# Gate stage of a decoder layer: the last chunk of each embedding product in column halves, a step's weights fetched a step sooner, another order in the last step

## The chip, the cores and the metric

The kernel runs on one core of one Trainium2 chip. The metric is the device time of one execution in microseconds (us); lower is better. TensorE (PE) multiplies matrices, VectorE (DVE) and ScalarE (ACT) do elementwise work, SyncE's queue (SP) issues the DMAs of the stage looked at here.

## The reference

One layer of a hybrid decoder, 512 tokens of width 1024, all in fp32. After a projection, an attention branch, a recurrence and their merge, the layer adds an output projection to the residual and then a gated embedding. The change touches only that last part:

```python
h = h + merged.astype(dt) @ w_out[i]
ple = (p[i] @ w_ple[i]).astype(f32) * jax.nn.sigmoid((h @ w_ple_gate[i]).astype(f32))
h = h + ple.astype(dt)
```

Here `p` is 512x256, `w_ple` 256x1024 and `w_ple_gate` 1024x1024.

## The kernel before, in words

Everything is kept transposed: 128 features on the partitions, 512 tokens along the free axis. An fp32 product is made of three passes in the faster float32r form: each operand is split into a high part (a rounded copy, made by ACT) and a low part (the rest, a subtraction on DVE), and TensorE sums high x high, high x low and low x high.

The **gate stage** is the loop at L1067. It takes the product of `h` with the gate weights by a 2x2 block scheme with seven block products in place of eight (Winograd's form of Strassen's). The two blocks of tokens are the column halves `left` and `right` of 256, the two blocks of the contraction are chunks 0 to 3 and 4 to 7, and each of the four steps `p` makes output chunks `p` and `p + 4`. In a step there are four PSUM banks `a`, `b`, `c`, `d` (tiles ga, gb, gc, gd in the trace) and seven calls of `product` (L1081), each with 12 matmuls over 256 columns: a, b, c, d, then the accumulating ones that I call a', c' and d' (the second into banks a, c and d). The sums of these blocks and the gates go through tiles `uv`, `sa` (output chunk p) and `sb` (output chunk p + 4) on DVE.

The **embedding product** of a step is `embed(0)` and `embed(1)` (L1077), one for each output chunk: two contraction chunks of 128, three passes each, so six matmuls over 512 columns into a bank `pe`. `gated` (L1093) multiplies the gate by `pe`, adds `hf` (the residual sum `h`), and issues the store of the output.

**Order.** TensorE's order is the program's. DVE, ACT and SP work of this stage passes through `arith`, `act` and `load`, and `pin` (L184) ties each such instruction behind the one before it on its engine: all three engines run in program order, and an instruction that waits holds up everything behind it on its engine. What is left over of a step (`rest`: the last gate of chunk p + 4 and both `gated`) is done in the next step. The last step (`last`, p = 3) has no next one: it makes the gates and stores half by half (L1151 to L1161).

**Weights.** `Quadrants(p)` holds a step's gate weights. Its method `first` loads 512 KB into a tile `gr` (L960), `second` loads two tiles of 256 KB, `gra` and `grb` (L965; for p = 0 one tile `gs` instead). `gr` has the tag `w` with two buffers: `gr` of step 2 takes the place of `gs`, and `gr` of step 3 the place of `gr` of step 1. `prepare` makes the block sums and the splits of the next step's weights (tiles `ws`, `gra`, `s1` to `s4`, `22`, `gwh`, `gwl` in the trace, an `h` or `l` behind the name for high and low) during the step before. `Embedding(p)` loads 256 KB of embedding weights into `pw` and splits them into `pwh` and `pwl`.

In step p the kernel before calls `Quadrants(p + 2).second()` and `Embedding(p + 2)` at the start (L1073, L1075), but `thirdW.first()` at the end (L1178), behind `rest[1]()` and `rest[2]()`, which issue the two stores of step p - 1.

Of the kernel before, what the change touches and what calls it, by code (L numbers as in the profile page):

```python
# [18 lines left out]
S = 512  # L19
# [41 lines left out]
def hybrid_layer_kernel(  # L61
# [16 lines left out]
    V, A, G, PE = nc.vector, nc.scalar, nc.gpsimd, nc.tensor  # L78
# [11 lines left out]
    def unit(tag, name, dt=F32, shape=(128, 512)):  # L90
        return sb.tile(list(shape), dt, tag=tag, bufs=BUFS[tag], name=name)

    def bank(tag, name):
        return psum.tile([128, 512], F32, tag=tag, bufs={"mm": 4, "g": 2, "a": 2}[tag], name=name)
# [12 lines left out]
    def run_due():  # L107
        again = True
        while again:
            again = False  # L110
            for s_ in list(sides):
                w = s_[0]
                if callable(w):
                    if not w():
                        continue
                elif w > now[0]:
                    continue
                again = True
                try:
                    y = next(s_[1])  # L120
                    s_[0] = y if callable(y) else now[0] + y
                except StopIteration:
                    sides.remove(s_)

    def tick(us):
        now[0] += us
        run_due()
# [121 lines left out]
    def mm3(ps, wh, wl, xh, xl, kn, us=0.227):  # L249
        n, tot = 0, 3 * kn  # L250
        for k in range(kn):
            for a, b in ((wh, xh), (wh, xl), (wl, xh)):
                PE.matmul(ps, a[:, k, :], b[k], start=(n == 0), stop=(n == tot - 1))  # L253
                n += 1
            tick(3 * us)
# [626 lines left out]
    for n in range(KD):  # L882
# [3 lines left out]
        h_ = unit("YB", f"mh{n}", R)  # L886
        l_ = unit("A", f"ml{n}", R)
# [6 lines left out]
    left, right, lo4, hi4 = slice(0, HALF), slice(HALF, S), slice(0, 4), slice(4, 8)  # L894

    def arith(dst, a, b, op):
        pin(V.tensor_tensor(dst, a, b, op=op))  # L897

    def add(dst, a, b):
        arith(dst, a, b, OP.add)  # L900

    def sub(dst, a, b):
        arith(dst, a, b, OP.subtract)

    def act(dst, src, f=AF.Copy, scale=1.0):
        pin(A.activation(dst, src, f, scale=scale), "A")
# [6 lines left out]
    def load(dst, src):  # L913
        pin(nc.sync.dma_start(dst, src), "S")
# [112 lines left out]
    ph, pl, pws = [], [], []  # L1027
    for at, n in enumerate(PAIRS):
# [24 lines left out]
        if at in (2, 3):  # L1053
            t = unit("A", f"pf{at}")
# [12 lines left out]
    for p in range(4):  # L1067
        pes = [bank("ag"[p % 2], f"pe{p}{i}") for i in range(2)]
        a, b, c, d = (bank("mm", f"g{i}{p}") for i in "abcd")
        uv, s0, s1 = (unit("YB", f"{i}{p}") for i in ("uv", "sa", "sb"))  # L1070
        u, v = uv[:, left], uv[:, right]
        last = p == 3
        thirdW = Quadrants(p + 2).second() if p < 2 else None  # L1073
        if p < 2:
            pws.append(Embedding(p + 2))  # L1075

        def embed(i, cols=slice(0, S)):  # L1077
            h_, l_ = pws[p].halves
            mm3(pes[i][:, cols], h_[:, i], l_[:, i], [t[:, cols] for t in ph], [t[:, cols] for t in pl], 2)

        def product(dst, i, j, begin=True):  # L1081
            n = 0
            for k in range(4):
                bh, bl = B[j][k]
                for wt, bt in ((W[i][0], bh), (W[i][0], bl), (W[i][1], bh)):
                    PE.matmul(dst[:, left], wt[:, k, :], bt, start=begin and n == 0, stop=n == 11, skip_group_check=not begin)
                    n += 1
            tick(1.36)

        def gate(s, sign, cols):  # L1090
            act(s[:, cols], s[:, cols], AF.Sigmoid, sign)

        def gated(s, i, cols=slice(0, S), p=p, pes=pes):  # L1093
            arith(s[:, cols], s[:, cols], pes[i][:, cols], OP.mult)
            add(s[:, cols], s[:, cols], hf[p + 4 * i][:, cols])
            load(out[p + 4 * i][:, cols], s[:, cols])

        def first_of_1(u=u, d=d, s1=s1):
            add(s1[:, left], u, d[:, left])
            gate(s1, -1.0, left)  # L1100

        def first_of_0():
            product(a, "12", "21", False)
            act(s0[:, left], a[:, left], AF.Sigmoid)

        def second_of_0():
            product(c, "s4", "22", False)
            add(s0[:, right], u, c[:, left])
            gate(s0, 1.0, right)

        def second_of_1():
            add(s1[:, right], v, d[:, left])
            gate(s1, -1.0, right)

        def prepare(what, *names):
            if not last:
                getattr(nextW, what)(*names)

        if p == 0:
            embed(0)  # L1120
            embed(1)
        else:
            rest[0]()
        product(a, "11", "11")
        act(u, a[:, left])
        prepare("highs", "22")
        prepare("sums", "s3", "s1")
        if p:
            prepare("sums", "s2")
        product(b, "s2", "t2")  # L1130
        sub(u, u, b[:, left])
        prepare("highs", "r0", "s1", "s3")
        if p:
            prepare("lows", "22")
            embed(1 if last else 0)
            if last:
                rest[1]()
        product(c, "s1", "t1")
        add(v, u, c[:, left])
        if last:  # L1140
            embed(0, right)
            rest[2]()
        elif p:
            embed(1)
        else:
            prepare("sums", "s2")
        prepare("highs", "s2")
        prepare("lows", "r0")
        product(d, "s3", "t3")
        second_of_1()  # L1150
        if last:  # L1151
            gated(s1, 1, right)
            second_of_0()
            gated(s0, 0, right)
            product(d, "22", "t4", False)
            first_of_1()
            gated(s1, 1, left)
            first_of_0()
            embed(0, left)
            gated(s0, 0, left)  # L1160
            break  # L1161
        prepare("lows", "s2", "s1")
        first_of_0()
        if p:
            rest[1]()
        second_of_0()
        prepare("sums", "s4")
        prepare("highs", "s4")
        prepare("lows", "s3")
        if p == 0:  # L1170
            prepare("lows", "22")
        prepare("lows", "s4")
        if p:
            rest[2]()
        if p < 2:
            pws[-1].high()
            pws[-1].low()
            thirdW.first()  # L1178
        product(d, "22", "t4", False)
        rest = (first_of_1, lambda s0=s0, gated=gated: gated(s0, 0), lambda s1=s1, gated=gated: gated(s1, 1))  # L1180
        W, nextW = nextW, thirdW
# [67 lines left out]
```

## Time and profile before

| | us |
|---|---|
| median of 3 runs (465.32 to 465.4) | 465.35 |
| the profiled execution's own time | 465.26 |
| its span, first to last instruction | 463.3 |
| start of the gate stage (first pe matmul) | 407.18 |
| start of the last step (its product a) | 445.63 |
| last matmul of the span starts | 458.55 |
| last DVE instruction starts | 460.24 |

Start times are counted from the start of the span. In a row of the timeline the columns are: start, duration, engine, line, operation, output<-inputs, shape, count; a bracket at the end gives the engine's idle time before the row and what ended it. The duration of a matmul is longer than its distance to the next one, because matmuls overlap: the pace is read from the starts. Nearly every DVE instruction of the stage has line L897 and every ACT instruction L906, the helpers, so tiles tell them apart, not lines.

### The profile page before, as it was taken

How to read it: one execution, taken by the hardware profiler on the slowest of the kernel's cores; microseconds unless marked ns; L12 is line 12 of the kernel's file. 1: busy time of each engine (PE TensorE's matmuls, PEld its weight loads, DVE VectorE, ACT ScalarE, POOL GpSimd, SP SyncE). 2: the span in 40 equal slices, each digit the busy share in tenths (PEclk: the TensorE clock that was granted, in tenths of full speed). 3: DMA queues.
4: the chain of work that ended last, by engine and by line, in shares of the span. 5: the costliest groups of instructions: out<-in, count | busy, mean ns of one | idle time of the engine just before them, and what ended most of it. 6: DMA issues, size and time to landing. Idle time of an engine off the chain costs nothing.

```text
span 463.3 us, 7630 instructions
## 1 busy us (share of the span) xinstructions
PE 456.1 (98%) x2882; PEld 385.1 (83%) x2882; DVE 352.4 (76%) x747; ACT 281.1 (61%) x506; POOL 13.2 (3%) x34
## 2 busy tenths in 40 slices
PE   8999999999999999999999999999999999999996
PEld 6888888888888888878887888888888888899995
DVE  4899568869979888987898575234559878898696
ACT  5856655667688876968686776465334444555331
POOL 1004000000000010000000000000000000000000
PEclk9999999999999999999999999999999999999999
DMA  7632223312433323131422333121324444380212
GB/s 242 224 137 90 93 94 104 118 49 97 153 92 127 125 58 121 73 115 48 115 91 92 115 91 115 46 69 47 113 76 142 169 129 157 123 273 3 91 42 95
DMA packets 19604, 50.43 MB, mean 109 GB/s; under 512 B 2416, under 2 KB 3312, under 8 KB 19568
## 3 DMA queue, kind: packets, MB, share of 16 engines
q1 hardware_dynamic: 19424, 49.95, 32.5%
q8 instruction: 22, 0.36, 0.3%
q14 instruction: 14, 0.11, 0.1%
q10 hardware_dynamic: 144, 0.01, 0.0%
HBM read 45.75 MB, written 2.10 MB: 103 GB/s over the span
## 4 chain that ended last, share of the span: by engine, by line
PE 88%; DVE 7%; DMA 2%; issue 1%; ACT 1%; SPq 0%; DVEq 0%; ACTq 0%
PE h L253 9%; PE gb L253 9%; PE ga L253 9%; PE ak L393 5%; PE ua L253 5%; PE bq L253 5%; PE ub L253 5%; PE bf L253 5%; PE aq L393 5%; PE ag L253 5%; PE bg L253 5%; PE av L393 5%; PE bi L393 4%; PE s L697 2%; PE pt L715 2%; DVE sa L897 1%
## 5 line engine op out<-in xcount | busy, mean ns | idle before, releaser
L236 ACT ACTIVATE wh<-wf 128x1024 fp32r<-128x1024 f32 (+1 forms) x70 | 67.3, 961 | 68.0 <-PE h L253 9.9
L237 DVE TENSOR_TENSOR wl<-wf,wh 128x1024 fp32r<-128x1024 f32 (+1 forms) x70 | 77.5, 1108 | 25.3 <-ACT wh L236 25.0
L253 PE MATMUL gb<-xh,wh 128*128 128x512 f32 x64 | 26.0, 407 | 0.0
L253 PE MATMUL ga<-xh,wh 128*128 128x512 f32 x64 | 25.7, 401 | 0.0
L253 PE MATMUL gb<-xh,wl 128*128 128x512 f32 x64 | 25.1, 393 | 0.0
L253 PE MATMUL gb<-xl,wh 128*128 128x512 f32 x64 | 25.0, 391 | 0.0
L253 PE MATMUL ga<-xh,wl 128*128 128x512 f32 x64 | 25.0, 391 | 0.0
L253 PE MATMUL ga<-xl,wh 128*128 128x512 f32 x64 | 25.0, 390 | 0.0
L253 PE MATMUL h<-mh,wh 128*128 128x512 f32 x64 | 24.9, 389 | 0.0
L253 PE MATMUL h<-mh,wl 128*128 128x512 f32 x64 | 24.9, 389 | 0.0
L253 PE MATMUL h<-ml,wh 128*128 128x512 f32 x64 | 24.9, 389 | 0.0
L704 DVE CUSTOM_DVE_ANT_0 p<-s,bias 128x128 f32<-128x128 f32 (+3 forms) x32 | 14.9, 485 | 12.9 <-PE s L697 12.9
L706 ACT ACTIVATE p<-p,ps 128x128 f32<-128x128 f32 (+3 forms) x32 | 17.7, 554 | 9.9 <-DVE ps L704 9.9
L719 ACT ACTIVATE ptS<-pt 128x384 f32<-128x384 f32 (+1 forms) x24 | 12.6, 523 | 11.8 <-PE pt L715 11.6
L253 PEld LDWEIGHTS gb<-xh,wl 128*128 128x128 f32 x64 | 12.0, 188 | 2.6
L253 PEld LDWEIGHTS ga<-xh,wl 128*128 128x128 f32 x64 | 12.0, 188 | 2.6
L253 PEld LDWEIGHTS h<-ml,wh 128*128 128x128 f32 x64 | 12.0, 188 | 2.6
L715 PE MATMUL pt<-ident,p 128*128 128x128 f32 x80 | 13.0, 276 | 1.1 <-DVE p L708 1.1
L253 PEld LDWEIGHTS h<-mh,wh 128*128 128x128 f32 x64 | 12.0, 188 | 2.5
L253 PEld LDWEIGHTS h<-mh,wl 128*128 128x128 f32 x64 | 12.0, 188 | 2.4
L253 PEld LDWEIGHTS ga<-xl,wh 128*128 128x128 f32 x64 | 12.1, 188 | 2.2
L253 PEld LDWEIGHTS ga<-xh,wh 128*128 128x128 f32 x64 | 12.0, 188 | 2.2
(411 smaller groups left out, 1403.4 us busy)
## 6 DMA issues: line engine op xcount, KB each, us to landing
wf<-in_w_tr_dram SPq DMA_DIRECT2D x32, 512.0 KB, 3.3
wf<-in_w_tok_dram SPq DMA_DIRECT2D x15, 512.0 KB, 3.3
wf<-in_w_up_dram SPq DMA_DIRECT2D x16, 256.0 KB, 2.5
wf<-in_w_o_dram SPq DMA_DIRECT2D x8, 512.0 KB, 3.3
bias<-in_brow_dram SPq DMA_DIRECT2D x8, 256.0 KB, 3.4
xres<-in_xT_dram SPq DMA_DIRECT2D x8, 256.0 KB, 3.0
gr<-in_w_g_dram SPq DMA_DIRECT2D x4, 512.0 KB, 4.7
xr<-in_xT_dram SPq DMA_DIRECT2D x7, 256.0 KB, 5.2
```

Source lines behind the costliest of these rows:

```text
L236: A.activation(hi, wraw[i], AF.Copy)
L237: pin(V.tensor_tensor(lo, wraw[i], hi.bitcast(F32), op=OP.subtract))
L253: PE.matmul(ps, a[:, k, :], b[k], start=(n == 0), stop=(n == tot - 1))
L393: PE.matmul(banks[t], a[:, s_], b[:, kk, :], start=(k == 0 and i == 0), stop=(k == KD - 1 and i == 2))
L697: PE.matmul(sp[:, o:o + nk], qn[h][:, qs], k_[:, :nk], start=(i == 0), stop=(i == 1))
L704: V.tensor_tensor_reduce(p_, sp[:, o:o + nk], T[:, nk - 1::-1], -1.0, 3e38, OP.add, OP.min, st[:, 0:1])
L706: A.activation(p_, p_, AF.Exp, bias=st[:, 0:1], scale=-1.0, accum_out=st[:, 1:2])
L715: PE.transpose(tp[:, kb * 128:kb * 128 + 128], pr[:, kb * 128:kb * 128 + 128], ident)
L719: A.activation(pt, tp[:, :n * 128], AF.Copy)
L897: pin(V.tensor_tensor(dst, a, b, op=op))
```

## The change: what it does

Three edits, all in the loop of the gate stage:

1. `embed` of a whole bank runs its first contraction chunk over 512 columns as before, and its second one over the left 256 columns (three passes) and then over the right 256 (three passes): nine matmuls in place of six. A call with one half given (`embed(0, right)`, `embed(0, left)`) does what it did.
2. `Quadrants(p + 2).first()` is called at the start of step p, ahead of `second()` and of `Embedding(p + 2)`, and no longer at its end.
3. In the last step TensorE's order a, b, E1, c, E0 right, d, c', d', a', E0 left becomes a, b, c, d, E1, c', d', E0 right, a', E0 left (E1 is `embed(1)`, E0 `embed(0)`). On DVE and SP `gated(s0, 0, right)` goes from before the last gate's sum (`first_of_1`) to behind it.

```diff
-        thirdW = Quadrants(p + 2).second() if p < 2 else None
+        thirdW = Quadrants(p + 2).first().second() if p < 2 else None
...
-        def embed(i, cols=slice(0, S)):
+        def embed(i, *parts):
+
             h_, l_ = pws[p].halves
-            mm3(pes[i][:, cols], h_[:, i], l_[:, i], [t[:, cols] for t in ph], [t[:, cols] for t in pl], 2)
+            for k in range(2):
+                for cols in parts or ((slice(0, S),), (left, right))[k]:
+                    for n, (wt, t) in enumerate(((h_, ph), (h_, pl), (l_, ph))):
+                        PE.matmul(pes[i][:, cols], wt[:, i, k, :], t[k][:, cols], start=k == n == 0,
+                                  stop=k == 1 and n == 2 and (bool(parts) or cols == right))
+            tick(1.36 if not parts else 0.68)
...
             prepare("lows", "22")
-            embed(1 if last else 0)
             if last:
                 rest[1]()
+            else:
+                embed(0)
         product(c, "s1", "t1")
         add(v, u, c[:, left])
         if last:
-            embed(0, right)
             rest[2]()
...
         second_of_1()
         if last:
+            embed(1)
             gated(s1, 1, right)
             second_of_0()
-            gated(s0, 0, right)
             product(d, "22", "t4", False)
             first_of_1()
+            embed(0, right)
+            gated(s0, 0, right)
             gated(s1, 1, left)
             first_of_0()
             embed(0, left)
...
             pws[-1].low()
-            thirdW.first()
         product(d, "22", "t4", False)
```

## Prediction

> **What bounds the kernel now.** I read the page first, then the chain that ended last from 400 us on, then the timelines of SP, PE and DVE through the gate stage. The page:
>
> ```profile
> span 463.3 us, 7630 instructions
> ...
> PE 456.1 (98%) x2882; PEld 385.1 (83%) x2882; DVE 352.4 (76%) x747; ACT 281.1 (61%) x506; POOL 13.2 (3%) x34
> ```
>
> TensorE is nearly always busy, with one weight load (PEld) for each matmul. So a change can save little more than PE's few gaps and what follows its last matmul. The chain gives PE's pace, and one stretch that isn't PE:
>
> ```profile
> 407.34 2.72 PE pe L253 x12
> ...
> 411.47 1.41 PE gb L1086 x12
> ...
> 435.03 0.34 SPq L914
> ...
> 435.43 3.66 DMA gr<-in_w_g_dram
> ...
> 439.18 0.70 DVE ws L897
> ```
>
> Pace: 2.72 / 12 = 0.227 us for a pass of 512 columns, 1.41 / 12 = 0.118 for one of 256; so a block product takes 1.41 and a whole embedding product 1.36. Further down, the end hangs on the load of step 3's `gr`: issued at 435.43 behind the store at 435.03, 3.66 us on the way, and DVE starts only then. DVE in order of time (the rows that I need):
>
> ```profile
> 428.37 0.42 DVE L897 TENSOR_TENSOR sb<-uv,gd 128x256 f32<-128x256 f32 x1 [1.22 <-PE gd L1086]
> ...
> 435.49 0.41 DVE L897 TENSOR_TENSOR sb<-uv,gd 128x256 f32<-128x256 f32 x1
> 439.18 0.69 DVE L897 TENSOR_TENSOR ws<-gr,gra 128x512 f32<-128x512 f32 x1 [3.28 <-DMA gr<-in_w_g_dram]
> ...
> 443.64 0.41 DVE L897 TENSOR_TENSOR sb<-uv,gd 128x256 f32<-128x256 f32 x1
> ...
> 446.51 0.41 DVE L897 TENSOR_TENSOR sa<-uv,gc 128x256 f32<-128x256 f32 x1
> ...
> 450.15 0.41 DVE L897 TENSOR_TENSOR sb<-uv,gd 128x256 f32<-128x256 f32 x1
> 451.33 0.42 DVE L897 TENSOR_TENSOR uv<-uv,gb 128x256 f32<-128x256 f32 x1 [0.76 <-ACT uv L906]
> ...
> 452.99 0.41 DVE L897 TENSOR_TENSOR uv<-uv,gc 128x256 f32<-128x256 f32 x1
> ...
> 454.64 0.41 DVE L897 TENSOR_TENSOR sb<-uv,gd 128x256 f32<-128x256 f32 x1
> 455.54 0.42 DVE L897 TENSOR_TENSOR sb<-sb,pe 128x256 f32<-128x256 f32 x1 [0.48 <-ACT sb L906]
> ...
> 456.34 0.41 DVE L897 TENSOR_TENSOR sa<-uv,gc 128x256 f32<-128x256 f32 x1
> 457.29 0.42 DVE L897 TENSOR_TENSOR sa<-sa,pe 128x256 f32<-128x256 f32 x1 [0.54 <-ACT sa L906]
> ...
> 458.09 0.41 DVE L897 TENSOR_TENSOR sb<-uv,gd 128x256 f32<-128x256 f32 x1
> 458.99 0.42 DVE L897 TENSOR_TENSOR sb<-sb,pe 128x256 f32<-128x256 f32 x1 [0.48 <-ACT sb L906]
> 459.44 0.43 DVE L897 TENSOR_TENSOR sb<-sb,hf 128x256 f32<-128x256 f32 x1
> 459.79 0.41 DVE L897 TENSOR_TENSOR sa<-sa,pe 128x256 f32<-128x256 f32 x1
> 460.24 0.42 DVE L897 TENSOR_TENSOR sa<-sa,hf 128x256 f32<-128x256 f32 x1
> ```
>
> DVE stands still for 3.28 us at 439.18 and is behind from there to the end. In step 1 it had waited 1.22 us for product d (428.37), so it was ahead of PE; in the last step it waits only for ACT's answers to its own sums (0.76, 0.48, 0.54, 0.48). PE beside it:
>
> ```profile
> 428.05 0.28 PE L1086 MATMUL gd<-tbh,s3l 128*128 128x256 f32 x1
> ...
> 440.66 0.28 PE L1086 MATMUL gd<-tbh,s3l 128*128 128x256 f32 x1
> ...
> 442.65 0.39 PE L1086 MATMUL gc<-hhh,s4h 128*128 128x256 f32 x1 [0.29 <-DVE uv L897]
> ...
> 445.63 0.28 PE L1086 MATMUL ga<-b11h,gwh 128*128 128x256 f32 x1
> ...
> 458.55 0.28 PE L253 MATMUL pe<-ph,pwl 128*128 128x256 f32 x1
> ```
>
> The last matmul of d starts at 428.05 and DVE reads d 0.32 later: I use 0.32 from the start of a bank's last matmul to its reader. In step 2 the reader comes at 443.64, 2.98 after 440.66. PE waits for DVE at 442.65, and after the last matmul (458.55) DVE still has 1.69 us to go until 460.24. So the last 25 us are bounded by DVE, late because of one load. The end follows the last DVE row by 463.3 - 460.24 = 3.06 us (store and close), which I keep.
>
> **The load of `gr` (edit 2).** What hinders an early load is its buffer, and what an early load may hinder stands behind it on SP:
>
> ```profile
> 409.53 0.37 SPq L914 DMA_DIRECT2D gr<-in_w_g_dram  x1
> 410.00 0.38 SPq L914 DMA_DIRECT2D gra<-in_w_g_dram  x1
> ...
> 411.38 0.33 SPq L914 DMA_DIRECT2D pw<-in_w_p_dram  x1
> ```
>
> ```profile
> 408.67 0.68 DVE L897 TENSOR_TENSOR 22l<-gs,22h 128x512 fp32r<-128x512 f32 x1
> ...
> 418.92 0.69 DVE L897 TENSOR_TENSOR ws<-ws,gr 128x512 f32<-128x512 f32 x1
> ...
> 422.26 0.69 DVE L897 TENSOR_TENSOR ws<-gr,gra 128x512 f32<-128x512 f32 x1
> ```
>
> ```profile
> 420.24 0.62 ACT L906 ACTIVATE pwh<-pw 128x512 fp32r<-128x512 f32 x1
> ...
> 432.82 0.61 ACT L906 ACTIVATE pwh<-pw 128x512 fp32r<-128x512 f32 x1
> ```
>
> ```profile
> DMA to landing us min/median/max: 5.7/6.3/6.5
> ```
>
> (The last line is that of the `grb` loads, the slowest of the stage.) `gr` of step 2 takes the buffer of `gs`, whose last reader ends at 408.67 + 0.68 = 409.35; it was issued at 409.53 already, and stays there. Now it goes first, and SP waits on it with `gra`, `grb` and `pw` of step 2 behind: the last goes out near 409.5 + 3 x 0.45 = 410.9 and is in by 417.4 even at 6.5 us. The first users are ACT at 420.24 (`pw`) and DVE at 422.26 (`gr`, `gra`): cover 2.8 and 4.9 us, so this costs nothing. `gr` of step 3 takes the buffer of step 1's, whose last reader ends at 418.92 + 0.69 = 419.61: issued near 419.7 in place of 435.43, with step 3's `gra`, `grb` and `pw` behind it until 421.1, all in by 427.6. ACT wants `pw` at 432.82, DVE wants `gr` at 435.83: covers of 5 and 8 us. Both stores of that step (the second at 435.03) now come behind these loads, which wait for nothing by then. So the 3.28 us stall goes.
>
> **What is late next, step 2.** Without the stall DVE goes on at 435.83 (435.49 plus the 0.34 that a short row takes when the next doesn't wait). From the stall's end to the sum from d it took 443.64 - 439.18 = 4.46, so it gets there by 440.3; what its rows there read from PE (b, c) and ACT is done before they come. Now d is late: PE's last matmul of d starts at 440.66 plus the price of edit 1. DVE reads d at 441.14 in place of 443.64: 2.50 earned, the rest of the 3.28 lost to waiting for PE.
>
> **Halves (edit 1).** A whole embedding product becomes 3 x 0.227 + 6 x 0.118 = 1.386 in place of 1.36: 0.026, and six of them (steps 0 to 2) before the last step make 0.16. No reader of `pe` comes so soon that a half done earlier helps it: the first one comes a step later, save in the last step. As bounds: nothing, if two halves run at 2 x 0.1135, and 3 x 0.188 us per product if the added weight loads lay open (a rival). I take 0.026, since each block product has 12 weight loads and 12 passes at the same 0.118.
>
> The Trainium skill (TensorE: Matmul & The Clock Gate, Back-to-back issue gap) gives N / 2.4 + 2.5 ns for a pass. By that a split adds 3 x 2.5 ns, 0.05 us over seven products and not 0.18, and the sum would come to 463.5; the trace's 227 and 118 ns are above its 216 and 109, and I go by the trace.
>
> **The last step.** PE without the wait at 442.65: a of step 3 starts at 440.82 + 0.118 + 3 x 1.413 = 445.18 (before 445.63, later by 0.61 of waiting). From there, by the new order: a, b, c, d end at 5.65, E1 at 7.04, c' at 8.45, d' at 9.87, E0 right at 10.57, a' at 11.99, E0 left at 12.69. The last matmul of each starts 0.12 before: d' 454.93, E0 right 455.63, a' 457.05, E0 left 457.75.
>
> DVE from 441.14, by the distances of the rows before (same instructions in the same order): the sum `sa` from c' of step 2 at +2.87, 444.01 (c' is readable at 440.82 + 24 x 0.118 + 0.32 = 443.97, so this just fits); `sb` at +6.51, 447.65; then from 450.15 as zero: `uv` from b +1.18, from c +2.84, `sb` from d +4.49 = 452.14, times `pe` +5.39 = 453.04 (E1 is done at 452.2), `sa` from c' +6.19 = 453.84 (c' readable at 453.83). All of it is ahead of d'. Now PE leads: `sb` from d' at 454.93 + 0.32 = 455.25 (DVE free since 454.2), `sa` times `pe` at 455.95, plus `hf` 456.41, `sb` times `pe` 456.75 (ACT's gate was ready at 455.25 + 0.90), plus `hf` 457.20, `sa` times `pe` at 457.75 + 0.32 = 458.07, plus `hf` at **458.52**. Before: 460.24. So edit 3 puts a DVE pair into ACT's pause after d', and DVE is free 0.5 us before the last multiplication: the end is PE-bound.
>
> **Sum.** 458.52 + 3.06 = 461.58 of span, 1.72 less; the execution 465.26 - 1.72 = 463.54, and against the median, 0.09 above that execution, **463.6**. In terms: 0.61 of PE's waits in step 2 gone, 0.16 of halves paid, the other 1.27 from the last step, where PE no longer waits and DVE no longer trails.
>
> **Rivals.**
>
> A: the load doesn't come sooner (its buffer or SP holds it to the old time) or another wait takes its place, and DVE reaches 450.15 as before. Then edit 3 alone acts: `uv` from c at 452.99 and `sb` from d at 454.64 hold c' and d' back as now, d' is read at about 456.8, `sa` times `pe` right at 457.4, E0 left starts its last matmul at 459.2, and the last row comes at 460.0: 465.1, no change. For it: DVE must still do as much. Against it: the buffer's reader ends at 419.61, 16 us before the old issue.
>
> B: the added weight loads lie open. One takes 188 ns:
>
> ```profile
> L253 PEld LDWEIGHTS pe<-ph,pwh x18: 187/188/192, 407.0 to 458.2; 128*128 128x128 f32 x18
> ```
>
> 21 of them (three in each of seven products) would cost 3.9 us on PE, and 463.6 - 0.2 + 3.9 = 467.3 comes out. It decides from 0.09 us per load on (1.9 / 21). Against it: block products with a 188 ns load for each pass go at 118 ns. The Trainium skill (TensorE: Matmul & The Clock Gate, The mechanism) says that weight loads overlap matmuls in flight only where their row groups differ, which would make this so; the trace doesn't bear it out for full 128 rows.
>
> C, slower too: SP waits for the buffer of `gs` with `pw` of step 2 behind it, and `pw` lands late. ACT then stands at 420.24, and behind it in order every gate and split of step 1. DVE makes up 1.22 (428.37) and the 3.28 of the stall that is gone; so the end is later only for a landing past about 425.2, 14 us after the issue. At 427 it would be 1.8 later less edit 3's 0.24, 466.9. Against it: 6.5 us is the longest landing.
>
> **How the numbers follow.** Forecast 0.84, A 0.10, B 0.03, C 0.03. The prediction is 463.6. Low end 463.2: the last step's 96 passes at half of 0.227 save 0.4. High end 464.6: a point between forecast and A, where some of DVE's 2.50 is lost to a wait that I don't see. A change under 0.2% (0.93 us) can't be told from none here: faster 0.84, same 0.10, slower 0.06.
>
> **What would show it.** In the changed profile: `gr` of step 3 issued near 419.7; DVE's wait before `ws` gone and one for PE before the sum from d at about 441.1; no wait of c' in step 2; a of the last step near 445.2; the last DVE row 0.77 after the last matmul's start, not 1.69; nine `pe` matmuls in about 1.39. Wrong if DVE waits for a DMA anywhere in the stage, if DVE is behind PE at d' of the last step, or if pe passes of 256 columns come slower than 0.118.

## The result, and the profile after

The changed kernel takes 462.29 us (median of 6 runs, 461.83 to 462.54) against 465.40 of the kernel before on the same chip: ratio 0.9932, 95% interval 0.992 to 0.9944. It is faster, as forecast, but by 3.1 us and not by 1.8: the time lies below the range on record.

The page of the changed kernel:

```profile
span 460.4 us, 7677 instructions
...
PE 454.5 (99%) x2903; PEld 384.7 (84%) x2903; DVE 352.2 (76%) x747; ACT 280.9 (61%) x506; POOL 13.1 (3%) x34
```

There are 21 matmuls more, three in each of seven embedding products, and yet PE's busy time is 1.6 us less. The SP queue's timeline:

```profile
409.39 0.33 SPq L914 DMA_DIRECT2D gr<-in_w_g_dram  x1
...
410.71 0.43 SPq L914 DMA_DIRECT2D pw<-in_w_p_dram  x1
...
419.50 0.33 SPq L914 DMA_DIRECT2D gr<-in_w_g_dram  x1
...
420.83 0.43 SPq L914 DMA_DIRECT2D pw<-in_w_p_dram  x1
```

These are the loads where the prediction put them (409.5, 410.9, 419.7 and 421.1), each within 0.3 us. DVE's timeline, the rows that answer to those of before:

```profile
435.10 0.41 DVE L897 TENSOR_TENSOR sb<-uv,gd 128x256 f32<-128x256 f32 x1
435.43 0.69 DVE L897 TENSOR_TENSOR ws<-gr,gra 128x512 f32<-128x512 f32 x1
...
440.36 0.42 DVE L897 TENSOR_TENSOR sb<-uv,gd 128x256 f32<-128x256 f32 x1 [0.39 <-PE gd L1092]
...
454.02 0.42 DVE L897 TENSOR_TENSOR sb<-uv,gd 128x256 f32<-128x256 f32 x1 [0.56 <-PE gd L1092]
454.80 0.42 DVE L897 TENSOR_TENSOR sa<-sa,pe 128x256 f32<-128x256 f32 x1 [0.35 <-PE pe L1083]
...
456.88 0.42 DVE L897 TENSOR_TENSOR sa<-sa,pe 128x256 f32<-128x256 f32 x1 [0.41 <-PE pe L1083]
457.33 0.42 DVE L897 TENSOR_TENSOR sa<-sa,hf 128x256 f32<-128x256 f32 x1
```

The 3.28 us stall before `ws` is gone, DVE waits for product d of step 2 instead, and in the last step for PE three times (d', E0 right, E0 left). The end is PE-bound: the last DVE row comes 0.84 us after the start of the last matmul (0.77 was forecast):

```profile
456.49 0.28 PE L1083 MATMUL pe<-ph,pwl 128*128 128x256 f32 x1
```

All of this is the walk on record, only earlier. How much earlier shows in the chain that ended last (start, us, what):

```profile
422.37 1.41 PE pe L1083 x9
423.78 1.38 PE gc L1092 x12
425.16 1.41 PE pe L1083 x9
426.57 1.38 PE gd L1092 x12
427.95 1.36 PE ga L1092 x12
```

A halved embedding product takes 1.41 us, about what was forecast (1.39). But a block product takes 1.36 to 1.38, where it took 1.41 before: 12 passes at 113 to 115 ns on average in place of 118. Nothing in the block products was edited.

To compare single profiles without the drift of the start, I use below the **stage length**: from the start of the first `pe` matmul to the start of the last DVE row. Before: 460.24 - 407.18 = 53.06. Forecast: 458.52 - 407.18 = 51.34. Changed: 457.33 - 407.15 = 50.18.

### The profile page after: what moved, and what is told of

Read it like the earlier page. It is cut to its first block, busy times and chain, and to the rows that moved or that the text cites. A ratio compares the mean times of both kernels' runs of the same rounds, so it can differ in the third digit from the quotient of the medians.

```text
span 460.4 us, 7677 instructions
## 1 busy us (share of the span) xinstructions
PE 454.5 (99%) x2903; PEld 384.7 (84%) x2903; DVE 352.2 (76%) x747; ACT 280.9 (61%) x506; POOL 13.1 (3%) x34
## 4 chain that ended last, share of the span: by engine, by line
PE 95%; DVE 2%; DMA 1%; SPq 0%; issue 0%; ACT 0%; DVEq 0%
PE h L253 9%; PE gb L253 9%; PE ga L253 9%; PE ak L393 5%; PE ua L253 5%; PE bq L253 5%; PE ub L253 5%; PE bf L253 5%; PE aq L393 5%; PE ag L253 5%; PE bg L253 5%; PE av L393 5%; PE bi L393 4%; PE pe L1083 2%; PE gc L1092 2%; PE gd L1092 2%
## 5 line engine op out<-in xcount | busy, mean ns | idle before, releaser
L253 PEld LDWEIGHTS gb<-xl,wh 128*128 128x128 f32 x64 | 12.1, 188 | 2.1
```

## The experiments

Each ran beside the kernel before on the same chip. That kernel's median differs a little from one group of runs to another (465.04 to 465.43), so each row has its own.

| run | us | before | ratio, 95% interval | stage length | block products (most) |
|---|---|---|---|---|---|
| changed kernel | 462.29 | 465.40 | 0.9932 (0.992 to 0.9944) | 50.18 | 113 |
| e1_no_halves | 463.05 | 465.04 | 0.9955 (0.9942 to 0.9967) | 51.20 | 118 |
| e2_halves_alone | 464.90 | 465.04 | 0.9999 (0.999 to 1.0008) | 52.74 | 113 |
| e3_load_alone | 463.23 | 465.04 | 0.9958 (0.9945 to 0.9972) | 51.33 | 118, from d of the last step on 113 |
| e4_order_alone | 465.05 | 465.04 | 0.9997 (0.9988 to 1.0005) | 53.02 | 118 |
| e5_first_chunk | 463.54 | 465.43 | 0.996 (0.9948 to 0.9973) | 51.52 | 118 |
| e6_last_pass | 462.25 | 465.43 | 0.9932 (0.992 to 0.9945) | 50.01 | 113 |
| e7_right_left | 462.12 | 465.43 | 0.993 (0.9918 to 0.9943) | 50.18 | 113 |
| e8_step0_only | 463.05 | 465.43 | 0.9957 (0.9943 to 0.997) | 50.83 | 113, then 118 |
| e9_load_halves | 462.48 | 465.12 | 0.9945 (0.9933 to 0.9958) | 50.46 | 113 |
| e10_last_384 | 462.38 | 465.12 | 0.9945 (0.9932 to 0.9957) | 50.37 | 113 |
| e11_other_passes | 463.26 | 465.12 | 0.9962 (0.9948 to 0.9975) | 51.20 | 118 |
| e12_first_twice | 463.88 | 465.12 | 0.9972 (0.9961 to 0.9982) | 51.90 | 118 |
| e13_all_halves | 462.28 | 465.17 | 0.9939 (0.9925 to 0.9952) | 50.32 | 113 |
| e14_first_cut | 462.43 | 465.17 | 0.9948 (0.9936 to 0.9961) | 50.53 | 113, c' and d' of the last step 118 |

The last column is the pace in ns per pass of the block products, from the starts in PE's timeline, once a run of passes has settled. In every run a' of the last step goes at 113; in the new order it stands directly behind E0 right, an embedding product in half columns.

### One edit taken away, one edit alone

**e1_no_halves**: edits 2 and 3 only.

```diff
-            for k in range(2):
-                for cols in parts or ((slice(0, S),), (left, right))[k]:
+            for cols in parts or (slice(0, S),):
+                for k in range(2):
```

> The changed kernel with edit 1 undone: each embedding product again six passes of 512 columns (load sooner and new order kept). Theory P (the halves change the pace: behind a product that ends in passes of 256 columns the block products go at 113 ns a pass, behind one that ends in passes of 512 at 118): block products back at 0.118, 28 x 12 x 0.0044 = 1.5 us more on PE less 0.2 for the halves: 463.4 to 463.6 us, the forecast's walk without its halves. Rival Q (the pace comes from the load or the order, or by chance from the layout of the code): pace stays 0.113, about 462.2 us. Rival R (halves only cost, 0.026 each, and PE's gain came from elsewhere): 462.1 us.

**e2_halves_alone**: the kernel before with the new `embed` and nothing else.

> The kernel before with edit 1 alone. Theory P: block products at 0.113 in all of the stage, but DVE still stands for the late load of gr, which hangs on the stores of step 1, and these come 0.4 us sooner as PE does: about 465.0 us (464.7 to 465.2), PE waiting for DVE in steps 2 and 3. Rival Q: pace 0.118, 465.5 us. Rival R: 465.4 to 465.6 us.

**e3_load_alone**: the kernel before with one call moved.

```diff
-        thirdW = Quadrants(p + 2).second() if p < 2 else None
+        thirdW = Quadrants(p + 2).first().second() if p < 2 else None
...
-            thirdW.first()
```

> The kernel before with edit 2 alone. All theories but Q: DVE's 3.28 us stall gone, pace 0.118, about 463.4 to 463.6 us by the same walk as the forecast's with the old order of the last step. Rival Q, if the load sets the pace: 462.2 us.

**e4_order_alone**: the kernel before with the last step's new order and products of whole passes.

> The kernel before with edit 3 alone (embedding products in passes of 512). The forecast's case A: DVE is as late as before, 0.24 us off the tail, 465.1 us, pace 0.118. Rival Q, if the order sets the pace: products of the last step at 0.113, but DVE-bound, 465.0 us.

**e9_load_halves**: edits 1 and 2 with the old order.

> Edits 1 and 2 with the old order of the last step. If the load and the halves are all that counts: as the changed kernel, within 0.2 us (3.1 under before). If the new order is needed once PE is quicker (the forecast's walk of the tail: DVE then has ACT's pause after d' to itself again): 0.2 to 0.5 us slower than the changed kernel.

Measured: without the halves 1.99 us under before, and the block products are back at 1.41, as the chain of e1_no_halves shows:

```profile
406.91 2.72 PE pe L1083 x12
409.63 1.41 PE ga L1091 x12
411.05 1.41 PE gb L1091 x12
```

Its stage length is 51.20; the walk on record without its halves gives 51.34 - 0.18 = 51.16. So the load and the order did what was forecast, and the whole miss is edit 1: 50.18 - 51.20 = -1.02 where +0.18 was forecast. Q and R fall.

The load alone gives 1.81 of these 1.99 us; the new order alone nothing that can be told from none, as case A had it (0.24 forecast). With the load, the new order takes another 0.13 off the stage without halves (51.33 to 51.20) and 0.28 with them (50.46 to 50.18, within the 0.2 to 0.5 expected of e9_load_halves). The DVE rows of the old order show why it gains less from a quicker PE; the first read of d in the last step and the last row, in e3_load_alone and then in e9_load_halves:

```profile
452.52 0.42 DVE L897 TENSOR_TENSOR sb<-uv,gd 128x256 f32<-128x256 f32 x1 [0.35 <-PE gd L1086]
...
458.12 0.42 DVE L897 TENSOR_TENSOR sa<-sa,hf 128x256 f32<-128x256 f32 x1
```

```profile
451.85 0.42 DVE L897 TENSOR_TENSOR sb<-uv,gd 128x256 f32<-128x256 f32 x1 [0.33 <-PE gd L1092]
...
457.44 0.42 DVE L897 TENSOR_TENSOR sa<-sa,hf 128x256 f32<-128x256 f32 x1
```

From d on the old order needs 5.60 and 5.59 us: DVE and ACT set the end, and the pace of c', d' and a' doesn't count. In the new order PE sets it. The differences of 0.13 and 0.28 are read in single profiles and are below what the medians can tell.

The halves alone are worth nothing, though the block products go at 113 there too: DVE's row in e2_halves_alone says why.

```profile
439.04 0.69 DVE L897 TENSOR_TENSOR ws<-gr,gra 128x512 f32<-128x512 f32 x1 [3.34 <-DMA gr<-in_w_g_dram]
```

With the load as late as before, the stage is DVE-bound from there on, and what PE gains it spends waiting for DVE. So the edits are not additive: 0 alone, 1.0 behind the load.

### What of the halves sets the pace

**e5_first_chunk**, **e6_last_pass** and **e7_right_left** change which passes of an embedding product are cut (k is the chunk, n the pass within it):

```diff
# e5_first_chunk
+ todo = [(0, n, c) for c in (left, right) for n in range(3)] + [(1, n, whole) for n in range(3)]
# e6_last_pass
+ todo = [(k, n, whole) for k in range(2) for n in range(3)][:5] + [(1, 2, left), (1, 2, right)]
# e7_right_left
+ todo = [(0, n, whole) for n in range(3)] + [(1, n, c) for c in (right, left) for n in range(3)]
```

> The changed kernel with the first chunk of each embedding product in halves and the second one whole: as many passes, but the last three before the block products are of 512 columns. Theory P1 (what stands last before the block products sets their pace): they go at 0.118, E0 right of the last step alone makes a' fast; about 463.2 us, 0.2 above e1_no_halves. Rival P2 (any passes of 256 columns in the embedding product do it, or a longer code): 0.113, 462.3 us. Rival L (layout of the code, the number of instructions): as P2, since it has the same number.

> The changed kernel with only the last of an embedding product's six passes in halves (seven matmuls in place of nine). P1: block products at 0.113, and 7 x 2 x 0.01 = 0.15 us less for halves: 462.1 us. If two passes of 256 columns are too few to set the pace (theory P3: some eight or nine are needed, since the first fast pass in the changed kernel is the tenth): 0.118 and 463.0 us. Rival L: pace could be either, since the number of instructions differs.

> The changed kernel with the halves in the other order, right before left. P1 and P2: no change, 462.3 us. Rival H (the pace comes from the half of the bank that was written last: right half, then the block product in the left half): pace 0.118, 463.2 us.

The chain of e5_first_chunk, and then that of e6_last_pass:

```profile
406.85 2.81 PE pe L1087 x18
409.66 1.42 PE ga L1096 x12
411.08 1.41 PE gb L1096 x12
```

```profile
407.18 2.76 PE pe L1087 x14
409.94 1.38 PE ga L1096 x12
411.32 1.36 PE gb L1096 x12
```

As many passes as in the changed kernel, but with the long ones last, leave the block products slow (P2 and L fall); one pass cut in two, if it is the last, makes them fast (P3 falls); the half that is written last doesn't matter (H falls). P1 stands as far as these three runs go: what counts is what stands just before the block products. e6_last_pass has the shortest stage, 0.17 less than the changed kernel, about the 0.15 that its 14 fewer matmuls were expected to save; by the medians the two can't be told apart.

**e8_step0_only** keeps the halves in step 0 and whole passes from step 1 on.

> The changed kernel with halves in step 0 alone, whole products of six passes of 512 columns from step 1 on. P1: the block products of step 0 and a, b of step 1 at 0.113, all from c of step 1 on at 0.118 again until E0 right of the last step: 9 x 12 x 0.0044 = 0.5 us better than e1_no_halves less 0.05 for halves, about 462.6 us. If the state once set is kept (theory P4): 0.113 to the end, 462.2 us.

```profile
420.69 1.36 PE gb L1096 x12
422.05 1.38 PE pe L1087 x6
423.43 1.41 PE gc L1096 x12
```

The rows are b of step 1, E0 with whole passes, and c: fast until the first pass of 512 columns, slow behind it. A fast state isn't kept (P4 falls); the stage is 0.37 shorter than that of e1_no_halves, where 0.45 was expected.

**e10_last_384** (the last pass as 384 and 128 columns), **e11_other_passes** and **e12_first_twice** (both from e1_no_halves):

```diff
# e10_last_384
+ todo = [...][:5] + [(1, 2, slice(0, 384)), (1, 2, slice(384, S))]
# e11_other_passes
-                for wt, bt in ((W[i][0], bh), (W[i][0], bl), (W[i][1], bh)):
+                for wt, bt in ((W[i][0], bh), (W[i][1], bh), (W[i][0], bl)):
# e12_first_twice, for the products behind an embedding product
+            if twice:
+                PE.matmul(dst[:, left], W[i][0][:, 0, :], B[j][0][0], start=True, stop=True)
```

> The changed kernel with an embedding product's last pass cut into 384 and 128 columns (as e6_last_pass with other widths). Theory W1 (any cut between the last pass of 512 columns and the block products breaks the slow pace): 113 ns, the same as e6_last_pass. Theory W2 (the pass before a block product must have its width, 256): 118 ns, 463.2 against 465.3 before.

> e1_no_halves with the three passes of a block product in another order (high x high, low x high, high x low), so that no weight is loaded twice running inside a chunk. If the slow pace comes from loading the same weight twice running: 113 ns in all block products and about 462.0 us. Else 118 ns and 463.1, as e1_no_halves (2.0 under before).

> e1_no_halves with the first pass of each block product that stands directly behind an embedding product given twice (five extra passes; the second one starts the sum anew, so the result is the same). Theory W1: an extra pass with the same weights between 512 columns and the rest breaks the slow pace: 113 ns in steps 0 to 2 and about 462.2 against 465.3 before. Theory W3 (only passes into the embedding's own bank do it): 118 ns, 463.1 plus 5 x 0.118 = 463.7.

The widths needn't match (W2 falls): 384 and 128 do it too, with a rougher first product (1.43). The order of the weights has no part in it. An extra pass of 256 columns behind the boundary changes nothing; the chain of e12_first_twice:

```profile
409.81 0.12 PE ga L1089
409.93 1.41 PE ga L1093 x12
411.34 1.41 PE gb L1093 x12
```

So W1 falls as it was put, and two readings were left: the short pass must be the embedding's (W3), or it must differ from the run of 256 columns that follows.

**e13_all_halves** (no pass of 512 columns in the stage) and **e14_first_cut** (whole embedding products, and the first pass of the block product behind each cut into 128 and 128 columns):

```diff
# e13_all_halves
+ todo = [(k, n, c) for k in range(2) for c in (left, right) for n in range(3)]
# e14_first_cut
+                    for q in (slice(0, 128), slice(128, HALF)) if cut and n == 0 else (left,):
```

> The changed kernel with both chunks of an embedding product in halves, twelve passes of 256 columns and no pass of 512 in the stage. Theory S (the slow pace is a state that the passes of 512 columns leave behind, and some nine short passes after a change of bank end it): block products at 113; the embedding's own passes begin at 118 and end at 113, 1.38 to 1.42 per product, about 462.3 (3.1 under before). Theory T (passes into the embedding's bank go at 118 whatever stands before): 12 x 0.118 = 1.42 per product, block products at 113, 462.4. If block products go at 118 again, three passes of 512 columns are needed ahead of the halves: 463.4.

> e1_no_halves with the first pass of each block product directly behind an embedding product cut into 128 and 128 columns. Theory W4 (any change of width to less than 256 columns between the 512 and the run of 256 ends the slow pace, whichever bank it writes): 113 in steps 0 to 2, about 462.2 (2.9 under before). Theory W3 (the short passes must stand ahead of the block product, as the last of the embedding's): 118, 463.1 to 463.3 (2.0 under before).

The chain of e13_all_halves and that of e14_first_cut:

```profile
407.18 2.87 PE pe L1087 x24
410.05 1.38 PE ga L1096 x12
411.43 1.36 PE gb L1096 x12
```

```profile
407.35 2.72 PE pe L1083 x12
410.07 1.48 PE ga L1092 x13
411.55 1.36 PE gb L1092 x12
```

In e13_all_halves the 24 short passes into `pe` go at 120 ns on average (2.87 / 24) and don't settle at 113: for them theory T holds, not S. The block products behind them are fast. In e14_first_cut the cut lies behind the boundary, in the block product's own bank, and the run behind it is fast (W4; W3 falls); c' of the last step, which was not cut, stays at 118. So neither the bank nor the place ahead of the boundary is needed. One rival is not separated: in every cut that worked, a short pass wrote columns that don't start at its bank's first one (the right half, the last 128 of 512, the second 128 of 256), while the extra pass of e12_first_twice wrote the same columns as the run behind it.

A cut isn't the only thing that changes the pace: a wait of PE can do it too. In e4_order_alone all embedding products of steps 0 to 2 are whole, and c' of step 2 comes after a wait for DVE (PE's timeline):

```profile
440.20 0.28 PE L1091 MATMUL ga<-hhh,gwh 128*128 128x256 f32 x1
...
441.50 0.28 PE L1091 MATMUL ga<-hhh,gwl 128*128 128x256 f32 x1
442.13 0.39 PE L1091 MATMUL gc<-hhh,s4h 128*128 128x256 f32 x1 [0.35 <-DVE uv L897]
...
442.70 0.28 PE L1091 MATMUL gc<-hhl,s4h 128*128 128x256 f32 x1
...
443.49 0.28 PE L1091 MATMUL gc<-hhh,s4l 128*128 128x256 f32 x1
443.61 0.37 PE L1091 MATMUL gd<-tbh,22h 128*128 128x256 f32 x1
443.81 0.28 PE L1091 MATMUL gd<-tbl,22h 128*128 128x256 f32 x1
...
444.99 0.28 PE L1091 MATMUL gd<-tbh,22l 128*128 128x256 f32 x1
```

a' goes at 118 ns (eleven distances in 1.30 us), c' settles at 113 (seven in 0.79), and d', whose second pass comes 0.20 us behind its first, is back at 118 (ten in 1.18, from 443.81 on). In the kernel before, the wait at 442.65 leaves the pace at 118. So a wait can end the slow pace, bring it back, or leave it; which of them isn't explained here. Where PE doesn't wait, all 16 traces keep to one rule: directly behind a pass of 512 columns the block products go at 118, behind a cut pass or an embedding product in half columns they settle at 113, and they stay there until the next embedding product.

## Why the prediction was wrong

**Right, with sizes.** The load: its queue slot, its buffer and its covers came within 0.3 us of the forecast, nothing behind it on SP came late (rival C didn't occur), and the load did not stay (rival A). The new bound: DVE waits for d in step 2, c' no longer waits, and the tail is PE-bound. Load and order together: 51.16 forecast, 51.20 measured in e1_no_halves. The added weight loads stay hidden: nine passes in 1.41 and not in 1.36 + 3 x 0.19 (rival B didn't occur). The Trainium skill (TensorE: Matmul & The Clock Gate, The mechanism) says that weight loads overlap matmuls in flight only where their row groups differ, and names beside it a background weight buffer that lets a load go ahead. No run here bears out the first as a limit: passes follow each other at 113 ns with a 188 ns load for each.

**Wrong: the step "Halves (edit 1)".** It gave the edit a price of 0.026 us per embedding product and no gain, "since each block product has 12 weight loads and 12 passes at the same 0.118", and took 0.118 as the block products' pace for the whole walk. The price held roughly: 1.386 forecast, 1.41 measured. The pace did not: the edit itself changes it. 28 block products at 1.36 (seven of them, each behind an embedding product, at 1.37 to 1.38) and not at 1.413 are 39.56 - (21 x 1.36 + 7 x 1.38) = 1.34 us less; seven embedding products cost 7 x 0.02 = 0.14 more than forecast; together 1.2, and the stage came out 51.34 - 50.18 = 1.16 shorter than forecast. The low end of the range allowed for passes at "half of 0.227" in the last step alone (96 passes, 0.4 us), so it ended at 463.2.

The trace before held the sign. In its last step, d and a' went at the fast pace (PE's timeline of the kernel before):

```profile
452.44 0.28 PE L1086 MATMUL gd<-tbl,s3h 128*128 128x256 f32 x1
...
453.23 0.28 PE L1086 MATMUL gd<-tbh,s3l 128*128 128x256 f32 x1
...
453.74 0.28 PE L1086 MATMUL gc<-hhl,s4h 128*128 128x256 f32 x1
...
454.92 0.28 PE L1086 MATMUL gc<-hhh,s4l 128*128 128x256 f32 x1
...
456.60 0.28 PE L1086 MATMUL ga<-hhh,gwh 128*128 128x256 f32 x1
...
457.85 0.28 PE L1086 MATMUL ga<-hhh,gwl 128*128 128x256 f32 x1
```

In d seven distances take 0.79 us (113 ns), in c' ten take 1.18 (118), in a' eleven take 1.25 (114). d stands directly behind E0 right, the one embedding product that was already in half columns; PE waited before c' and before d', so a' can't be put down to it. One instruction form with two paces in one trace was the row to ask about before taking one mean for all.

**What stays open.** Which part of TensorE keeps the two paces apart. The runs exclude the number of instructions (e5_first_chunk against e7_right_left), which half of the bank was written last, the order of weights and the bank of the short passes. They show the transition that sets the slow pace, not its mechanism, nor why a wait of PE changes the pace in some places.

## What to carry to other kernels

Read the pace of a repeated instruction from its starts, stage by stage, and ask why when one form has two; a mean over them hides what an edit next to it may change. Where a run of 256-column passes follows one of 512 columns directly, try cutting the last long pass (e6_last_pass: seven matmuls more than e1_no_halves and 1.19 us of stage less). The edit that quickens TensorE was worth nothing here while DVE bounded the stage: look for the late load first, then measure the edits together.

## What the runs showed of the hardware

Passes of 256 columns have three paces here, at a granted clock of 0.998 to 1.0 in the profiled execution of every run: 118 ns in a run that starts directly behind a pass of 512 columns, kept through up to nine block products (108 passes in the kernel before, from step 0 to b of step 1); 113 ns, half of a 512-column pass, when a cut pass or an embedding product in half columns stood between; and 117 to 120 ns on average for passes into the embedding's bank, whatever stood before. A wait of PE can switch a run between the first two (118 before it and 113 behind it in e4_order_alone, above). The Trainium skill (TensorE: Matmul & The Clock Gate, Back-to-back issue gap), quoted in the prediction, gives one gap for each width, and gives it for isolated matmuls. Here every pass has a weight load of its own, and the runs show 4% between two runs of the same instructions, by what stood before them.

Six passes of 512 columns took 1.36 us in the kernel before, but 1.38 behind fast block products (E0 of step 1 in e8_step0_only, above). That isn't a simple pairing either: in e12_first_twice, with slow block products, E0 of step 1 took 1.38 as well.

```profile
422.64 1.38 PE pe L1083 x6
```
